# A hybrid block on one core: the order of work at the joints of its stages

## The chip, the cores and the metric

One core of one Trainium2 chip. The metric is device time in microseconds (us) of one execution. A core has five engines that run beside each other and meet through semaphores: TensorE (PE, with its weight loads PEld), VectorE (DVE), ScalarE (ACT), GpSimd (POOL) and SyncE (SP, which only issues DMAs here).

## The reference

One transformer-like block over 512 tokens of width 2048, all in fp32:

```python
h = hybrid_mixer(x, ...)            # mLSTM in chunks, and forgetting attention with 16 heads
x = layer_norm(ALPHA * x + h, ...)
h = memory_cross_attention(x, mem, w_q, w_kv, w_o)
x = layer_norm(ALPHA * x + h, ...)
h = peer_ffn(x, w_pq, sub_keys, expert_u, expert_v)
x = layer_norm(ALPHA * x + h, ...)
```

In the mixer, `merged = sigmoid(g_ml) * (h @ w_br_ml) + sigmoid(g_fx) * (y @ w_br_fx)` gates the two branches with projections of x. In `peer_ffn` each token scores two sets of 128 keys in 8 heads, picks 16 of the 16384 experts for each head (a top 16 of sums of two top 16s), softmaxes their scores to g, and computes `sum_k gelu(u_k . x) * g_k * v_k`.

## The kernel before

**Precision and the weight ring.** Every large matmul is done in three fp32r passes: hi x hi, hi x lo, lo x hi. A weight tile of 128 x 2048 floats (1 MB) is loaded by SP into a buffer `raw` (`load_raw`, L161), cast to its high part in two halves on ACT (L182), and VectorE subtracts to get the low part (L185). Both parts stand in a slot of the `ring`; later there are two slots. `shares` does this and calls the `ticks`. `group_ws` (L206) and `group_as` (L248, L249, L256) are generators that stop after every weight tile, so that another generator can be advanced in between (`mix`, `take`). A group uses three or four of five PSUM banks `mm`.

**The planner.** The instructions of an engine run in an order that a planner sets before the run: it takes those that are ready in its own reckoning of time, and among these the earlier in the program's text first. `after(i, j)` forces i behind j on their engine without a semaphore, and `ring["gate"]`, when set, puts L185 of each tile that follows behind an instruction.

**The stages.** The first 128 tokens go through the mixer, cross attention and key selection first, mixed with the products of the memory (`mem_stage`). Then 384 tokens go through the mLSTM (`second`, which starts with four groups of gates, `ml1_gates`, with raw buffers from its own pool `mlg` beside the weights' pool `wp`) and through `fx1`: four quads of four attention heads each (`fox_head`), with the q, k and v groups of the next quad after them in the program, and after the last quad four groups of gates (w_in 28 to 31). Then the ends: block 1 and blocks 2 and 3 alternate between `residual`, `norm` and `attend`. `norm` takes a function `mid` that is called right behind its last statistic (L777); `behind(g, n)` makes one that advances another generator n weight tiles, all gated behind that statistic.

**The experts, two ways.** For tokens 0 to 255 the chosen rows of `peer_u` and `peer_v` are gathered with indirect DMAs (L1026), and VectorE does the dot products (L1046) and the sums (L1062). These are the `jobs`: each tile of weights earns credit, and a job is issued on POOL and used on VectorE two or three tiles later. For tokens 256 to 511 all experts are computed densely: `next_a` takes one tile of `uT` (128 experts, a U tile), computes their activations in 48 matmuls, and after every second tile a Gelu (L1334) writes a pair of them to `ga`. 28 pairs go to DRAM (`gad`) and come back as `gb`. A matrix G of the gates per expert is built with one-hot matmuls (L1386). `stage_h` multiplies a pair with its part of G (L1427), casts it to `hph` (L150) and subtracts to `hpl` (L151). `stage_o` then runs over 16 experts at a time and two halves dh of the columns: eight V tiles of `vD` with 24 matmuls each (L1467, L1468, L1464), and adds to `acc` at the end (L1479, L1481). From expert 56 on, one U tile follows each V tile (`fill`), until all 128 are done.

Selection (`Choice.run`, `select`) of the 256 dense tokens is eight steps of small operations on VectorE; three U tiles are issued beside each of the first seven, five beside the last.

Of the kernel before, what the change touches and what calls it, by code (L numbers as in the profile page):

```python
# [10 lines left out]
F32 = mybir.dt.float32  # L11
# [4 lines left out]
AF = mybir.ActivationFunctionType  # L16
# [5 lines left out]
P = 128  # L22
# [20 lines left out]
J = 16  # L43
# [6 lines left out]
def build(tc, I, out):  # L50
    nc = tc.nc
    NC_ = PKEYS
    with ExitStack() as ctx:
# [99 lines left out]
        def load_raw(src, n=2048):  # L153
# [7 lines left out]
            nc.sync.dma_start(raw[:, :n], src)  # L161
            return raw

        ring = {"n": 0, "tiles": [wp.tile([P, 4096], F32R, tag="ring", name="ring0")]}

        def add_ring(p):
# [2 lines left out]
        def shares(raw, cost, hold=None):  # L169

            wide = len(ring["tiles"]) > 1
            for i in range(1 if wide else 2):
                ring["n"] += 1
                if wide:
                    t = ring["tiles"][ring["n"] % len(ring["tiles"])]
                    hi, lo, src = t[:, 0:2048], t[:, 2048:4096], raw
                else:
                    t, o = ring["tiles"][0], (ring["n"] % 2) * 1024
                    hi, lo = t[:, o:o + 1024], t[:, 2048 + o:3072 + o]
                    src = raw[:, i * 1024:(i + 1) * 1024]  # L180
                for c in range(0, 2048 if wide else 1024, 1024):
                    x = nc.scalar.copy(hi[:, c:c + 1024], src[:, c:c + 1024])  # L182
                    if hold is not None:
                        after(x, hold)
                s = nc.vector.tensor_sub(lo, src, hi.bitcast(F32))  # L185
                if ring.get("gate") is not None:
                    after(s, ring["gate"])
                for f in ticks:
                    f(s, cost * (2 if wide else 1))
                yield (hi, lo, 0, 2048) if wide else (hi, lo, i * 1024, 1024)  # L190
# [454 lines left out]

        def fx1(X, ypool, yT, galloc, G):
            n = 384
            with pool("fxa", side="right") as fp:
                def ft(tag, bufs, n=512):
                    return fp.tile([P, n], F32, tag=tag, bufs=bufs, name=nm(tag))  # L650
# [44 lines left out]
                for qd in range(4):  # L695
                    qs, ks, vs = {}, {}, {}

                    def ev_q(s, b, qs=qs):
                        qs[s] = ft("c", 10, n)
                        nc.scalar.activation(qs[s], b, AF.Copy, scale=FX_D ** -0.5)  # L700

                    def ev_k(s, b, ks=ks):
                        ks[s] = ft("c", 10, n)
                        nc.scalar.copy(ks[s], b)

                    def ev_v(t, b, vs=vs):
                        vs[1 + t] = ft("v", 4)
                        nc.scalar.copy(vs[1 + t], b)

                    yield from group_ws(wi[16 + 3 * qd], X, 3, ev_q)  # L710
                    yield from group_ws(wi[17 + 3 * qd], X, 3, ev_k)
                    kp, vs[0] = ft("kp", 1), ft("vp", 1)
                    nc.sync.dma_start(kp, fxk[qd])
                    nc.sync.dma_start(vs[0], fxv[qd])
                    yield from group_as(wi[18 + 3 * qd], X, 3, ev_v)
                    for s in range(4):
                        fox_head(4 * qd + s, qs[s], ks[s], kp[:, s * P:(s + 1) * P], vs, s * FX_D)
            with pool("fxg", side="right") as fp:
                sgf = []

                def ev_g(s, b):
                    t = fp.tile([P, n], F32, tag="sg", bufs=16, name=nm("sg"))
                    nc.scalar.activation(t, b, AF.Sigmoid)
                    sgf.append(t)

                for g in range(4):
                    yield from group_ws(wi[28 + g], X, 3, ev_g)

                for g in range(4):
                    def ev_b(s, b, g=g):  # L730
                        m1 = fp.tile([P, n], F32, tag="m1", bufs=3, name=nm("m1"))
                        nc.sync.dma_start(m1, mg[g * 4 + s])
                        t = sgf[g * 4 + s]
                        nc.vector.tensor_mul(t, t, b)
                        nc.vector.tensor_add(t, t, m1)
                        a, l = galloc()
                        split(a, l, t)
                        G.append((a, l))

                    yield from group_ws(I["w_br_fx"][g], yT, 3, ev_b)  # L740
# [273 lines left out]


        jobs = []
        state = {"done": 0, "credit": 0.0, "rate": 0.0, "later": [], "n": 0, "lag": 3, "mult": 1.0}
        gat = {}
        tok = {}

# [105 lines left out]
            for _ in range(n):  # L1126
                next(g, 0)

        def behind(g, n):

            def mid(last):
                ring["gate"] = last
                take(g, n)
                ring["gate"] = None

            return mid
# [66 lines left out]

        def second():
            with pool("mlg", side="right") as gp:
                raws["pools"] = [wp, gp]
                yield from ml1_gates(gp, X)
                raws["pools"] = [wp]
            yield from ml1(mls.enter_context(pool("ml1", side="right")), X, prB, hT)

# [45 lines left out]
        cs = ExitStack()  # L1256
        cpl = cs.enter_context(pool("x1c", side="right"))
        res = e1.residual(PTb, Bv, False)
        e2.norm(0, X1c, lambda: pair(cpl, "X", 16), False, behind(res, 3))
        att = e2.attend(X1c, pr1, PTc)  # L1260
        mix(res, att, 2)
        e1.norm(1, X2b, pr1, True, behind(att, 2))
# [1 line left out]
        with pool("pick1") as pp:  # L1264
# [13 lines left out]
            next(cr)  # L1278

            def mid(last):  # L1280
                c.gate = ring["gate"] = last
                take(cr, 3)
                ring["gate"] = None

            e2.norm(1, X2, lambda: pair(fpl, "X", 16), True, mid)
# [24 lines left out]
        def next_a(hold=None):  # L1310
# [19 lines left out]
                    i = nc.tensor.matmul(bank, ul[:, sl], X2[k][0], start=False, stop=k == 15)  # L1330
            abank[1:] = [i]
            if c % 2:
                ga = gap.tile([P, 512], F32, tag="ga", bufs=GA, name=nm("ga"))
                nc.scalar.activation(ga, abank[0], AF.Gelu)  # L1334
                if c // 2 in spilled:
                    nc.scalar.dma_start(gad[c // 2], ga)
                else:
                    gas[c // 2] = ga

        raws["pools"], raws["one"] = [wp, rw, wp, rw, gap], gap  # L1340
        with pool("topk", side="right") as tp:
            c = Choice(pp, tp, 2)
            steps = 0
            for w in c.run(X2, nc.sync):
                if w:
                    steps += 1
                    for i in range(5 if steps == 8 else 3):
                        next_a(w[1] if i else None)
        sel = c.sel
        rws.close()  # L1350
# [69 lines left out]
        def stage_h(c):  # L1420
# [3 lines left out]
            gt = g4[c - c % 4][:, :, c % 4:c % 4 + 2]  # L1424
            ga = gas.pop(c // 2)
            gv = ga.rearrange("p (c b t) -> p c b t", c=2, t=64)
            nc.vector.tensor_mul(gv, gv, gt.rearrange("p b c t -> p c b t"))  # L1427
            a, b = pair(mn, "hp", J + 2)
            split(a, b, ga)
            hs[c], hs[c + 1] = parts(a, b, H)  # L1430
# [3 lines left out]
        def stage_o(c0, dh, fill):  # L1434
# [3 lines left out]
            for jj in range(J // 2):  # L1438
# [5 lines left out]
                    fin_load()  # L1444
                raw = load_raw(I["vD"][c0 // 2 + jj, dh])
                for vh, vl, o, w in shares(raw, 2.0):
                    for j in range(o // 1024, (o + w) // 1024):
                        c = c0 + 2 * jj + j
                        if dh == 0 and c % 2 == 0:
                            stage_h(c)  # L1450
                        if c0 == 0 and dh == 0 and c in (10, 12):
                            late(nc.sync.dma_start(acc[c // 2 - 5], x2d[HB + c // 2 - 5].rearrange("p g c -> p (g c)")))
                    js = range(o // 1024, (o + w) // 1024)
# [45 lines left out]
        while at[0] < ahead[0]:  # L1499
# [5 lines left out]
            if at[0] == ahead[0] - 1:  # L1505
                ask_g(4)
            next_a()
        for c0 in range(0, NC_, J):
            def fill(i, c0=c0):
                if i % 2:  # L1510
# [85 lines left out]
```

## Time and profile before

| | |
|---|---|
| three runs | 4623.32, 4625.78 (median), 4626.57 us |
| the profiled execution | 4626.68 us, span 4625.0 us, granted clock 0.987 |
| TensorE busy | 4472.6 us, 97% |
| VectorE, ScalarE, GpSimd busy | 3744.9, 2228.1, 855.8 us |
| DMA | 1488.70 MB, mean 322 GB/s |

In the profile, PE slices show how much of a stretch TensorE had a matmul in flight; the granted clock is a second figure, the share of its full speed that it was given. An idle time is given with the releaser that ended it.

Where the stages lie in the span: memory products and first block to 943.9 us; mLSTM and heads of the 384 tokens to 2295 (the last heads 2227 to 2295); gates and branch of the attention, then the ends, to about 2905; selection to 3200; G to about 3440; the last U tiles to 3509; V tiles without U tiles to 3844; V and U tiles to about 4515, V tiles to 4603.

### The profile page before, as it was taken

The page shows a single profiled execution, that of the slowest core. Times are in us where ns is not written, and L with a number is a line of the kernel's source. Part 1 is how long each engine was busy: PE and PEld are TensorE (multiplying, and loading weights), DVE is VectorE, ACT ScalarE, POOL GpSimd, SP SyncE. Part 2 cuts the span into 40 slices and gives each one's busy share as a digit, 9 for nine tenths or more (in the row PEclk, how much of TensorE's full clock was granted, in tenths as well). Part 3 has the DMA queues.
Part 4 walks back from the last instruction along what each step waited for, and adds up shares of the span by engine and source line. Part 5 has one row for each costly group of instructions (what it writes and reads, how often), then busy time and mean ns, then how long its engine had stood idle before and what let it go on. Part 6 is the DMA issues. An engine that isn't in the chain of part 4 may idle for free.

```text
span 4625.0 us, 65151 instructions
## 1 busy us (share of the span) xinstructions
PE 4472.6 (97%) x25702; PEld 3991.4 (86%) x25702; DVE 3744.9 (81%) x4326; ACT 2228.1 (48%) x3029; POOL 855.8 (19%) x631
## 2 busy tenths in 40 slices
PE   8999999999999999999999999898999999999998
PEld 7888888889888899999899777898997778888886
DVE  7877677647898887888779669799988998888888
ACT  6866776645343423333323575444763433343342
POOL 1000000000122222222131000111121223334332
PEclk9999999999999999999999999999999999999999
DMA  8898889656788899888699766786989999999897
GB/s 297 322 335 327 323 318 340 253 216 214 280 335 331 329 346 344 341 332 315 248 352 355 275 236 217 272 324 250 366 353 412 399 406 379 372 369 374 357 365 298
DMA packets 244019, 1488.70 MB, mean 322 GB/s; under 512 B 26588, under 2 KB 52252, under 8 KB 75392
## 3 DMA queue, kind: packets, MB, share of 16 engines
q1 hardware_dynamic: 150384, 888.47, 51.1%
q0 software_dynamic: 81664, 561.95, 31.0%
q10 hardware_dynamic: 11664, 34.12, 1.9%
q8 instruction: 201, 3.29, 0.3%
q14 instruction: 106, 0.87, 0.1%
HBM read 1425.15 MB, written 59.29 MB: 321 GB/s over the span
## 4 chain that ended last, share of the span: by engine, by line
PE 67%; DVE 5%; DMA 3%; issue 3%; ACT 2%; POOL 0%; DVEq 0%; ACTq 0%; SPq 0%; POOLq 0%
PE mm L206 22%; PE mm L256 6%; PE mm L249 6%; PE mm L248 6%; PE pa L1330 4%; PE mm L1467 4%; PE pa L1323 4%; PE pa L1326 4%; PE mm L1468 4%; PE mm L1464 4%; DVE ring L185 2%; DVE rows L1046 1%; ACT ring L182 1%; PE sm L689 1%; PE sm L623 1%
## 5 line engine op out<-in xcount | busy, mean ns | idle before, releaser
L182 ACT CAST ring<-raw 128x1024 fp32r<-128x1024 f32 x1568 | 1598.8, 1050 | 1482.8 <-PE mm L206 464.3
L185 DVE TENSOR_TENSOR ring<-raw,ring 128x2048 fp32r<-128x2048 f32 (+1 forms) x926 | 1813.4, 1962 | 509.0 <-ACT ring L182 226.7
L206 PE MATMUL mm<-Ah,ring 128*128 128x384 f32 x2560 | 673.5, 342 | 13.9 <-ACT Ah L150 11.5
L1026 POOL DMA_INDIRECT rows<-in_peer_u,ei x256 | 330.5, 1291 | 1674.4 <-DVE rows L1046 832.1
L1026 POOL DMA_INDIRECT rows<-in_peer_v,ei x256 | 458.6, 1791 | 968.8 <-DVE x2l L1062 713.4
L1046 DVE SCALAR_TENSOR_TENSOR rows<-rows,x2l 128x2048 f32<-128x2048 f32 x256 | 584.5, 2287 | 33.2 <-DMA rows<-in_peer_u,ei 33.0
L1062 DVE SCALAR_TENSOR_TENSOR x2l<-rows,dots,x2l 128x2048 f32<-128x2048 f32 x256 | 600.9, 2347 | 10.4 <-DMA rows<-in_peer_v,ei 10.1
L1323 PE MATMUL pa<-Xh,ring 128*128 128x256 f32 x2048 | 496.9, 284 | 4.8 <-ACT ring L182 4.7
L1326 PE MATMUL pa<-Xl,ring 128*128 128x256 f32 x2048 | 493.5, 282 | 0.0
L206 PEld LDWEIGHTS mm<-Ah,ring 128*128 128x128 f32 x2560 | 464.4, 189 | 19.6 <-ACT Ah L150 12.0
L1467 PE MATMUL mm<-ring,hph 128*128 128x512 f32 x1024 | 406.4, 397 | 32.2 <-ACT ring L182 30.0
L206 PE MATMUL mm<-Al,ring 128*128 128x384 f32 x1280 | 433.3, 341 | 0.0
L1468 PE MATMUL mm<-ring,hpl 128*128 128x512 f32 x1024 | 403.1, 394 | 0.0
L1323 PEld LDWEIGHTS pa<-Xh,ring 128*128 128x128 f32 x2048 | 388.1, 189 | 9.4 <-ACT ring L182 7.1
L1326 PEld LDWEIGHTS pa<-Xl,ring 128*128 128x128 f32 x2048 | 389.4, 190 | 2.2
L249 PE MATMUL mm<-ring,Zl 128*128 128x512 f32 x832 | 328.6, 395 | 0.0
L248 PE MATMUL mm<-ring,Zh 128*128 128x512 f32 x832 | 327.7, 394 | 0.8 <-ACT ring L182 0.8
L248 PE MATMUL mm<-ring,Ah 128*128 128x512 f32 x768 | 307.2, 400 | 1.1 <-ACT ring L182 1.1
L249 PE MATMUL mm<-ring,Al 128*128 128x512 f32 x768 | 304.4, 397 | 0.0
L1330 PE MATMUL pa<-Xh,ring 128*128 128x256 f32 x2048 | 266.3, 283 | 3.0 <-DVE ring L185 3.0
L1467 PEld LDWEIGHTS mm<-ring,hph 128*128 128x128 f32 x1024 | 193.2, 189 | 83.3 <-ACT ring L182 38.2
L206 PE MATMUL mm<-Bh,ring 128*128 128x384 f32 x1024 | 261.2, 338 | 0.7 <-DVE ring L185 0.7
(393 smaller groups left out, 7153.9 us busy)
## 6 DMA issues: line engine op xcount, KB each, us to landing
raw<-in_w_in SPq DMA_DIRECT2D x256, 1024.0 KB, 6.6
raw<-in_uT SPq DMA_DIRECT2D x128, 1024.0 KB, 8.3
raw<-in_vD SPq DMA_DIRECT2D x128, 1024.0 KB, 9.5
raw<-in_w_out SPq DMA_DIRECT2D x48, 1024.0 KB, 6.3
raw<-in_peer_wq SPq DMA_DIRECT2D x48, 1024.0 KB, 4.8
raw<-in_w_xkv SPq DMA_DIRECT2D x32, 1024.0 KB, 6.5
raw<-in_w_br_ml SPq DMA_DIRECT2D x32, 1024.0 KB, 7.0
raw<-in_w_br_fx SPq DMA_DIRECT2D x32, 1024.0 KB, 7.7
```

The costliest lines, as they stand in the source:

```text
L182: x = nc.scalar.copy(hi[:, c:c + 1024], src[:, c:c + 1024])
L185: s = nc.vector.tensor_sub(lo, src, hi.bitcast(F32))
L206: i = nc.tensor.matmul(o, w, x, start=start and s % per == 0, stop=stop and s % per == per - 1)
L248: nc.tensor.matmul(banks[t], xh[:, tt], wh[:, c], start=k == 0, stop=False)
L249: nc.tensor.matmul(banks[t], xl[:, tt], wh[:, c], start=False, stop=False)
L1026: i = nc.gpsimd.indirect_dma_start(out=rows, out_offset=None, in_=I[table], in_offset=bass.IndirectOffsetOnAxis(ap=ei[t][:, k:k + 1], axis=0))
L1046: i = nc.vector.scalar_tensor_tensor(rows, rows, 1.0, tok[t]["x2l"], op0=ALU.mult, op1=ALU.mult, accum_out=d[:, k % GB:k % GB + 1])
L1062: i = nc.vector.scalar_tensor_tensor(acc, rows, d[:, GB + k % GB:GB + k % GB + 1], acc, op0=ALU.mult, op1=ALU.add)
L1323: i = nc.tensor.matmul(bank, uh[:, sl], xh, start=k == 0, stop=False)
L1326: nc.tensor.matmul(bank, uh[:, sl], xl, start=False, stop=False)
L1467: nc.tensor.matmul(banks[t][g], a[:, tt], vh[:, gs_], start=c == c0, stop=False)
L1468: nc.tensor.matmul(banks[t][g], b[:, tt], vh[:, gs_], start=False, stop=False)
```

## The change

Six edits, all to order:

1. In `fx1` the first gate group (w_in 28) becomes a generator `g0`, begun before the heads. One of its weight tiles is issued ahead of each of heads 12, 13 and 14, the fourth behind head 15. Its Sigmoids still need the pool `fxg`, which opens after the heads.
2. `behind(g, n, free=1)` advances `free` tiles before the gate is set, and only the others behind it; one norm has `free` 2. The `mid` of the last norm does the same with one of its three tiles.
3. In `second` the first weight tile of `ml1_gates` is taken before the pool's raw buffers join.
4. In the main loop the Gelu of a pair is put on a list `put`, and issued behind the casts of the next weight tile.
5. `stage_h` runs one V tile ahead: the first pair before the loop, the first pair of the next 16 experts at the seventh V tile of the second half. Its multiply is forced behind the subtraction of the present V tile.
6. Seven U tiles instead of five are issued beside the last selection, and two fewer after G.

```diff
+        put = []
...
                     x = nc.scalar.copy(hi[:, c:c + 1024], src[:, c:c + 1024])
                     if hold is not None:
                         after(x, hold)
+                while put:
+                    put.pop(0)(x)
                 s = nc.vector.tensor_sub(lo, src, hi.bitcast(F32))
...
         def fx1(X, ypool, yT, galloc, G):
             n = 384
+            sgf, gate_pool = [], []
+            def ev_g(s, b):
+                t = gate_pool[0].tile([P, n], F32, tag="sg", bufs=16, name=nm("sg"))
+                nc.scalar.activation(t, b, AF.Sigmoid)
+                sgf.append(t)
+            g0 = group_ws(wi[28], X, 3, ev_g)
...
                     for s in range(4):
+                        if qd == 3 and s < 3:
+                            yield next(g0)
                         fox_head(4 * qd + s, qs[s], ks[s], kp[:, s * P:(s + 1) * P], vs, s * FX_D)
-            with pool("fxg", side="right") as fp:
...
-                for g in range(4):
+            with pool("fxg", side="right") as gp:
+                gate_pool.append(gp)
+                yield from g0
+                for g in range(1, 4):
                     yield from group_ws(wi[28 + g], X, 3, ev_g)
...
-        def behind(g, n):
+        def behind(g, n, free=1):
             def mid(last):
+                take(g, free)
                 ring["gate"] = last
-                take(g, n)
+                take(g, n - free)
                 ring["gate"] = None
...
             with pool("mlg", side="right") as gp:
+                g = ml1_gates(gp, X)
+                yield next(g)
                 raws["pools"] = [wp, gp]
-                yield from ml1_gates(gp, X)
+                yield from g
...
-        e2.norm(0, X1c, lambda: pair(cpl, "X", 16), False, behind(res, 3))
+        e2.norm(0, X1c, lambda: pair(cpl, "X", 16), False, behind(res, 3, 2))
...
             def mid(last):
-                c.gate = ring["gate"] = last
-                take(cr, 3)
+                c.gate = last
+                take(cr, 1)
+                ring["gate"] = last
+                take(cr, 2)
                 ring["gate"] = None
...
             if c % 2:
-                ga = gap.tile([P, 512], F32, tag="ga", bufs=GA, name=nm("ga"))
-                nc.scalar.activation(ga, abank[0], AF.Gelu)
-                if c // 2 in spilled:
-                    nc.scalar.dma_start(gad[c // 2], ga)
+                def evac(x, pa=abank[0]):
+                    ga = gap.tile([P, 512], F32, tag="ga", bufs=GA, name=nm("ga"))
+                    i = nc.scalar.activation(ga, pa, AF.Gelu)
+                    if x is not None:
+                        after(i, x)
+                    if c // 2 in spilled:
+                        nc.scalar.dma_start(gad[c // 2], ga)
+                    else:
+                        gas[c // 2] = ga
+                if state["put"]:
+                    put.append(evac)
                 else:
-                    gas[c // 2] = ga
+                    evac(None)
...
-                    for i in range(5 if steps == 8 else 3):
+                    for i in range(7 if steps == 8 else 3):
                         next_a(w[1] if i else None)
...
-            nc.vector.tensor_mul(gv, gv, gt.rearrange("p b c t -> p c b t"))
+            i = nc.vector.tensor_mul(gv, gv, gt.rearrange("p b c t -> p c b t"))
+            after(i, state["s"])
...
                 for vh, vl, o, w in shares(raw, 2.0):
+                    nxt = c0 + 2 * jj + 2 if dh == 0 else c0 + J
+                    if nxt < c0 + J or (dh and jj == 6 and not last):
+                        stage_h(nxt)
                     for j in range(o // 1024, (o + w) // 1024):
                         c = c0 + 2 * jj + j
-                        if dh == 0 and c % 2 == 0:
-                            stage_h(c)
...
             next_a()
+        while put:
+            put.pop(0)(None)
+        stage_h(0)
+        state["put"] = True
         for c0 in range(0, NC_, J):
```

`state["s"]` is the subtraction (L185) of the weight tile that was issued last.

More of the change, by code (lines that the diff above doesn't have):

```diff
@@ L716, in fx1 @@
                     for s in range(4):
+                        if qd == 3 and s < 3:
+                            yield next(g0)
                         fox_head(4 * qd + s, qs[s], ks[s], kp[:, s * P:(s + 1) * P], vs, s * FX_D)
-            with pool("fxg", side="right") as fp:
[L719 to L724, printed above, removed]
-                for g in range(4):
+            with pool("fxg", side="right") as gp:
+                gate_pool.append(gp)
+                yield from g0
+                for g in range(1, 4):
                     yield from group_ws(wi[28 + g], X, 3, ev_g)
@@ L730, in ev_b @@
                     def ev_b(s, b, g=g):
-                        m1 = fp.tile([P, n], F32, tag="m1", bufs=3, name=nm("m1"))
+                        m1 = gp.tile([P, n], F32, tag="m1", bufs=3, name=nm("m1"))
                         nc.sync.dma_start(m1, mg[g * 4 + s])
@@ L1016, in build @@
         jobs = []
-        state = {"done": 0, "credit": 0.0, "rate": 0.0, "later": [], "n": 0, "lag": 3, "mult": 1.0}
+        state = {"done": 0, "credit": 0.0, "rate": 0.0, "later": [], "n": 0, "lag": 3, "mult": 1.0, "put": False}
         gat = {}
```

## The prediction

> **What bounds the kernel now.** I read the page first, then the busy time by stretches wherever TensorE's slices fell short of full, then the idle groups and the order of time around each gap.
>
> ```profile
> PE 4472.6 (97%) x25702; PEld 3991.4 (86%) x25702; DVE 3744.9 (81%) x4326; ACT 2228.1 (48%) x3029; POOL 855.8 (19%) x631
> ...
> PEclk9999999999999999999999999999999999999999
> DMA  8898889656788899888699766786989999999897
> ```
>
> TensorE is the bound almost everywhere, so an edit is worth the idle time of TensorE that it takes away, and what half clock follows a gap. The stretches in which the gaps of this change lie (columns: window, its length, then busy time of PE, PEld, DVE, ACT, POOL, then granted clock, DMA share, GB/s):
>
> ```profile
> 943.90:955.40 11.50, 0.00 (x0) 0.00 (x0) 2.29 (x1) 1.44 (x4) 1.07 (x2) 0.67 0.75 269
> 955.40:975.10 19.70, 19.66 (x97) 19.66 (x98) 8.10 (x13) 8.83 (x15) 0.00 (x0) 0.85 0.52 190
> 2227.00:2272.50 45.50, 45.50 (x266) 42.93 (x265) 37.30 (x52) 15.72 (x29) 9.57 (x8) 1.00 0.84 305
> 2272.50:2295.40 22.90, 15.77 (x67) 10.05 (x65) 10.16 (x37) 8.86 (x22) 0.94 (x1) 0.85 0.37 125
> 2698.30:2704.00 5.70, 0.01 (x1) 0.00 (x0) 5.22 (x14) 4.29 (x7) 0.00 (x0) 0.85 0.00 0
> 2704.00:2711.00 7.00, 7.00 (x20) 5.55 (x21) 6.18 (x6) 5.25 (x7) 0.00 (x0) 0.64 0.81 302
> 2882.70:2887.30 4.60, 0.00 (x1) 0.01 (x1) 4.12 (x12) 2.43 (x5) 0.00 (x0) 0.92 0.00 0
> 2887.30:2894.00 6.70, 6.70 (x16) 4.97 (x16) 3.97 (x5) 2.80 (x4) 0.00 (x0) 0.55 0.84 313
> 3181.00:3200.50 19.50, 1.43 (x3) 0.54 (x3) 19.33 (x84) 4.16 (x10) 0.00 (x0) 0.56 0.21 87
> 3440.00:3509.00 69.00, 65.71 (x552) 65.10 (x550) 50.44 (x39) 26.49 (x36) 12.32 (x11) 1.00 1.02 421
> 3509.00:3844.00 335.00, 319.79 (x1346) 251.57 (x1347) 305.51 (x263) 130.78 (x152) 74.85 (x56) 0.99 1.01 405
> 3931.00:4488.50 557.50, 539.46 (x3461) 489.99 (x3461) 469.78 (x260) 217.54 (x240) 206.54 (x92) 1.00 0.92 367
> ```
>
> The reader should see three sorts of gap: five to twenty us at stage joints, each followed by a granted clock well under 1; a stretch from 3440 to 3844 where the DMA engines are never idle; and 557 us at the end where neither DMA nor VectorE is full and TensorE still loses 18.
>
> **The change part by part.** The sum is made against the profiled execution: 4626.68 us around a span of 4625.0; the median of the three runs is 4625.78, so what comes out may be compared with it as it stands.
>
> *Gelu behind the next tile's casts.* Here is one of the waits in the last stretch: the group of idle time, then ACT, PE and the load of that tile in order of time, and the usual landing time.
>
> ```profile
> L1467 PE MATMUL mm<-ring,hph 128*128 128x512 f32 x408 | 160.4, 393 | 17.8 <-ACT ring L182 17.8
> ...
> 3911.47 0.60 ACT L1334 ACTIVATE ga<-pa 128x512 f32<-128x512 f32 x1 [11.91 <-PE pa L1330]
> 3911.96 1.98 ACT L182 CAST ring<-raw 128x1024 fp32r<-128x1024 f32 x2
> ...
> 3913.05 0.50 PE L1467 MATMUL mm<-ring,hph 128*128 128x512 f32 x1 [1.62 <-ACT ring L182]
> ...
> 3895.62 0.34 SPq L161 DMA_DIRECT2D raw<-in_vD  x1
> ...
> raw<-in_vD SPq DMA_DIRECT2D x128, 1024.0 KB, 9.5
> ```
>
> ACT stood 11.91 us before a Gelu that needed the end of the U tile, with the casts of the next V tile queued behind it, although that tile's load, issued at 3895.62, lands by the usual 9.5 us at about 3905. TensorE then waits 1.62 us for 0.5 of Gelu and one cast of 1.0. The group says 17.8 us in 11 such waits (17.8 / 1.62). The edit fixes the order: casts first. What is queued behind the Gelu then are the U tile's casts, which need the ring slot that the same U tile frees, so they lose 0.5 us of the 5.6 us of V matmuls that cover them; the Gelu's bank and its result are wanted a whole pair of tiles later. The raw buffer also comes free some 6 us earlier, so SP's next load goes out sooner. Bounds: 0, if another order of the planner puts the same wait elsewhere, to 18. I take 18, since the wait has one cause each time and the cover is seen.
>
> *The first memory gate's tile before the new pool.*
>
> ```profile
> 919.91 0.33 SPq L161 DMA_DIRECT2D raw<-in_w_in  x1
> ...
> 948.59 0.80 SPq L161 DMA_DIRECT2D raw<-in_x1T  x2
> ...
> 954.88 1.34 ACT L150 CAST Ah<-raw 128x384 fp32r<-128x384 f32 x3 [10.06 <-DMA raw<-in_x1T]
> ```
>
> TensorE does nothing from 943.9 to 955.4 because both first pieces of x1T sit in raw buffers of the pool `mlg`, which is free only at 948.6, when the last stores of the stage before have landed. After the edit the first piece takes a buffer of the weights' pool, of which the next to come free takes a load at 919.91 now; the second piece still waits. So one step, 48 matmuls, runs in the gap: 48 x 45.5/266 = 8.2 us. The gap left is 11.5 - 8.2 = 3.3 us. The slow clock behind it cost 19.7 - 97 x 0.171 = 3.1 us; what a shorter gap costs is shown elsewhere:
>
> ```profile
> 3272.28 2.07 PE L1386 MATMUL mm<-o,o 128*128 128x128 f32 x8 [2.48 <-ACT o L1385]
> ...
> 3272.30:3275.60 3.30, 3.30 (x15) 3.30 (x16) 0.00 (x0) 3.30 (x7) 0.00 (x0) 0.50 0.97 407
> ```
>
> A gap of 2.48 us was followed by 3.3 us at half clock, that is 1.7 lost, so I keep 1.7 and win 8.2 + 1.4 = 9.6. [...] Moving the first piece forward also pushes one weight load back on SP. I take 9; bounds 4 (the memory of X itself comes free late) to 14.6 (gap and clock both gone).
>
> *One or two tiles outside the norm's gate.* In front of 2704 and 2887 the stretches lose 5.7 + 7.0 x 0.36 = 8.2 and 4.6 + 6.7 x 0.45 = 7.6 us.
>
> ```profile
> 2694.25 1.05 ACT L182 CAST ring<-raw 128x1024 fp32r<-128x1024 f32 x1 [1.79 <-PE mm L249]
> ...
> 2701.66 4.49 DVE L185 TENSOR_TENSOR ring<-raw,ring 128x2048 fp32r<-128x2048 f32 x2
> ```
>
> The second of two tiles was cast by 2695.3, but both subtractions stand behind the norm's last statistic and begin at 2701.66. Freed, they fit the holes VectorE has there or push the statistics back by at most one subtraction, 2.2 us. A tile for one block of 128 rows is 12 matmuls of 512; at 319.79/1346 = 0.24 us that is 2.9 us of cover. Two freed tiles cover the 5.7; one covers 2.9 of the 4.6. Work done early is missing later, but a subtraction fewer stands between the statistic and the normalisation, so the transposes come earlier too. I take 5 and 3; bounds -4 (two statistics chains pushed back by 2.2) to 15.8. The other norms have no such gap: 0.
>
> *Gate tiles between the last heads.* While heads 12 and 13 ran, the planner had already filled TensorE with all four steps of the first gate group (45.5 of 45.5 busy); heads 14 and 15 then ran bare, 22.9 us with 15.77 busy at clock 0.85. The edit puts three of the steps ahead of heads in program order. If the planner fills greedily again, the order only decides which heads run bare, and the first step, 8.2 us, now even stands in front of head 12. Three more weight loads pass heads' loads on SP. Bounds: -8.2 (a loss of one step) to +7 (the idle part gone). I take 0, because the same cover is there in both.
>
> *Seven keys beside the last selection.* Two U tiles, 48 matmuls each, 2 x 48 x 65.71/552 = 11.4 us, move from the stretch that starts at 3440 into the 19.5 us in which TensorE waits for the selection. But VectorE has no hole there (19.33 of 19.50), and each tile brings it a subtraction and its share of jobs:
>
> ```profile
> L185 DVE TENSOR_TENSOR ring<-raw,ring 128x2048 fp32r<-128x2048 f32 x7 | 16.0, 2289 | 0.0
> L1046 DVE SCALAR_TENSOR_TENSOR rows<-rows,x2l 128x2048 f32<-128x2048 f32 x5 | 11.4, 2286 | 0.0
> ```
>
> That is 2 x (2.29 + 5/7 x 2.29) = 7.9 us by which the selection ends later. Their loads on SP and 1.4 gathers on POOL move too, into a window with DMA to spare. Net 11.4 - 7.9 = 3.5; bounds -7.9 (nothing saved later) to +11.4. I take 3.5.
>
> *Gated activations one V tile ahead.* Between 3505 and 3844 TensorE idles this much before V tiles:
>
> ```profile
> L1467 PE MATMUL mm<-ring,hph 128*128 128x512 f32 x449 | 180.6, 402 | 14.4 <-ACT ring L182 12.2 <-DVE acc L1479 1.8 <-DVE acc L1481 0.4
> ...
> L1464 PE MATMUL mm<-ring,hph 128*128 128x512 f32 x448 | 113.4, 395 | 3.4 <-DVE ring L185 3.3
> ```
>
> That is 17.8 us, most of it casts standing behind `hph`, which waits for the multiply with G. The edit puts the multiply behind the present tile's subtraction and uses it one tile later. But DMA is full here: 335 us x 405 = 135.7 MB, and the best long rate, 421 from 3440 to 3509, would need 322 us: at most 13 us to win. Between 0 and 13 I take 5, nearer the lower end, for the rate over seven stages was 405 and not 421. [...]
>
> Sum: 18 + 9 + 8 + 0 + 3.5 + 5 = 43.5; 4626.7 - 43.5 = 4583.
>
> **Rivals.**
> *The multiply becomes a chain.* Each `hph` now needs the subtraction of the tile before, a job of 2.2 us stands between, and if the planner leaves `hph` ahead of the next tile's casts on ACT, every V tile with staging takes the whole round. It exists now:
>
> ```profile
> 3527.49 1.99 ACT L182 CAST ring<-raw 128x1024 fp32r<-128x1024 f32 x2
> 3534.65 0.62 ACT L150 CAST hph<-ga 128x512 fp32r<-128x512 f32 x1 [5.17 <-DVE ga L1427]
> 3535.17 1.99 ACT L182 CAST ring<-raw 128x1024 fp32r<-128x1024 f32 x2
> ...
> 3529.51 2.29 DVE L185 TENSOR_TENSOR ring<-raw,ring 128x2048 fp32r<-128x2048 f32 x1 [1.20 <-ACT ring L182]
> 3531.72 2.28 DVE L1046 SCALAR_TENSOR_TENSOR rows<-rows,x2l 128x2048 f32<-128x2048 f32 x1
> 3533.93 1.29 DVE L1427 TENSOR_TENSOR ga<-ga,G 128x512 f32<-128x512 f32 x2
> ```
>
> From cast to cast 7.7 us, against 5.7 for the 24 matmuls of a V tile. A first half then takes 7 x 7.7 + 5.7 = 59.6 us against 335/7 = 47.9 now: +11.7 for each of the four without U tiles, and 2 us for some six tiles more: +59 in place of -5, thus 4626.7 - 38.5 + 59 = 4647. It decides when about 19 of 34 tiles fall so (38.5 / 2). For it: the planner did put `hph` first here. Against: with the product ready a tile early, the casts have a tile's time of slack.
>
> *DMA holds the stretch from 3440.* The V stages keep their 335 us, and the two U tiles less save only their bytes, 3.6 MB / 421 = 8.5 against 7.9. Then 35.6 is won: 4591. For it: share 1.01 to 1.02. Against: stalls that have nothing to do with a landing.
>
> *The Gelu edit moves casts that were not ready.* If half of the V tiles land after the U tile's last matmuls, 9 of the 18 stay: 4592. Against it stands the load above.
>
> **How the numbers follow.** Forecast 0.57, DMA 0.20, Gelu 0.08, chain 0.15. 0.2% (9.3 us) is about what a measurement of this kernel can tell from no change. The first three are all faster; from their 0.85 I take 0.04 for a shuffle by the planner that turns them into a loss, so faster is 0.81. The chain's 0.15 is split: nearly complete it is slower (0.08, with the shuffle 0.12), about half complete it is within 0.2% (0.07). The range runs from 4563, with 20 us more from the norms, the join at 955, the heads and the V stretch, to 4613, which takes in DMA, Gelu and the head's loss of 8 together and part of a chain; beyond it lies most of the chain.
>
> **What would show it.** Gelu: the idle group of L1467 in the last stretch falls from 17.8 to under 3, casts stand ahead of each Gelu. Join: x1T once at about 920, TensorE's gap before 955 near 3 us. Norms: gaps of 5.7 and 4.6 under 2. Heads: bare stretch of about 23 us still there. Selection: TensorE's wait ends 8 us later relative to its start, two U tiles fewer after 3440. V stretch: seven stages in about 330 us. I am wrong if V tiles from 3509 come 7.7 us apart, if the last 557 us do not shrink, or if stages that the diff doesn't name grow.

## The result, and the profile after

| | time | beside the kernel before | ratio, 95% interval |
|---|---|---|---|
| changed kernel, first set | 4594.6 us (median of 6, 4586.8 to 4602.5) | 4627.9 | 0.9930 [0.9917, 0.9943] |
| changed kernel, second set | 4596.3 us (median of 5, 4593.5 to 4601.0) | 4624.1 | 0.9941 [0.9927, 0.9955] |

It is 28 to 33 us faster. (Below, a gain in us that stands beside a ratio is what the ratio gives; the difference of the medians lies up to 4 us beside it.) The forecast was 4583, the range 4563 to 4613. Two executions were profiled: one of 4602.5 us (span 4600.8, the slowest of its six) and one of 4599.3 (span 4597.6). The page of the first has these lines for the three shown of before:

```profile
PE 4467.5 (97%) x25702; PEld 3993.3 (87%) x25702; DVE 3743.1 (81%) x4326; ACT 2231.7 (49%) x3029; POOL 871.0 (19%) x631
...
PEclk9999999999999999999999999899999999999998
...
DMA  8898889766798889888789766786989999999997
```

They are nearly the same: 24 us in 4600 don't show in 40 slices. The stretches show more (window, length, busy time of PE, PEld, DVE, ACT, POOL, granted clock, DMA share, GB/s), placed by the same instructions as before:

```profile
944.30:955.30 11.00, 9.19 (x52) 8.74 (x52) 4.58 (x2) 4.83 (x6) 1.08 (x2) 1.00 0.89 289
955.30:966.00 10.70, 10.70 (x51) 9.71 (x50) 4.56 (x6) 5.49 (x9) 0.00 (x0) 0.84 0.97 377
2272.50:2296.40 23.90, 16.77 (x68) 10.63 (x67) 9.93 (x35) 9.03 (x22) 0.17 (x1) 0.86 0.30 110
2701.60:2708.40 6.80, 4.73 (x19) 3.36 (x19) 6.32 (x16) 5.99 (x8) 0.00 (x0) 1.00 0.56 170
2876.00:2885.50 9.50, 4.67 (x17) 2.90 (x16) 8.83 (x17) 4.39 (x7) 0.00 (x0) 0.93 0.59 221
2911.60:2924.50 12.90, 0.01 (x1) 0.01 (x1) 2.77 (x5) 2.23 (x5) 1.25 (x1) 0.63 0.89 340
...
3496.50:3834.60 338.10, 322.77 (x1345) 258.21 (x1346) 303.32 (x262) 131.78 (x151) 86.22 (x56) 0.97 0.99 399
3921.30:4455.70 534.40, 532.54 (x3431) 485.92 (x3430) 465.43 (x257) 218.27 (x240) 185.84 (x92) 1.00 0.95 381
4574.40:4600.80 26.40, 0.49 (x3) 0.05 (x1) 22.49 (x45) 0.61 (x3) 0.00 (x0) 0.55 0.29 119
```

The gap at 944 is filled (TensorE is busy for 9.19 of 11.0). The last long stretch, which lost 18 us of 557, loses 1.9 of 534. The heads' bare stretch is as it was. Of the norms' gaps 2.1 us (6.80 - 4.73) and 4.8 (9.50 - 4.67) are left, in several pieces. New are 12.9 us at 2911 in which TensorE does nothing, a V stretch of 338 us instead of 335, and an end of 26.4 us.

The whole difference, taken between the same instructions in each profile (lengths in us; "again" is the second profile of the changed kernel, "predicted" the change that the prediction's terms give, and the last column is a better kernel, told below):

| from one event to the next | before | after | again | predicted | best1 |
|---|---|---|---|---|---|
| start to the first matmul of the memory gates | 955.4 | 944.4 | 943.8 | -9 | 943.6 |
| to the first cast of the attention's branch at 1871 | 916.3 | 926.5 | 923.6 | 0 | 920.3 |
| to the last such cast (heads) | 421.3 | 423.1 | 423.0 | 0 | 422.7 |
| to the last norm's statistics | 590.0 | 585.3 | 585.3 | -5 | 585.1 |
| to the first Gelu | 73.3 | 72.6 | 72.5 | -3 | 63.1 |
| to the end of the selection | 241.0 | 247.6 | 247.4 | +8 | 247.9 |
| to the first V tile | 311.8 | 297.0 | 297.5 | -11.4 | 298.5 |
| seven stages of V tiles | 334.7 | 338.1 | 338.3 | -5 | 335.0 |
| seven stages of V and U tiles | 645.4 | 621.7 | 621.8 | -18 | 621.7 |
| two last stages | 114.2 | 118.1 | 118.0 | 0 | 117.4 |
| last accumulation to the end | 21.6 | 26.4 | 26.4 | 0 | 19.1 |

### The profile page after: what moved, and what is told of

Same layout as the page of the kernel before. It is cut to its first block, busy times and chain, and to the rows that moved or that the text cites. A ratio compares the mean times of both kernels' runs of the same rounds, so it can differ in the third digit from the quotient of the medians.

```text
span 4600.8 us, 65219 instructions
## 1 busy us (share of the span) xinstructions
PE 4467.5 (97%) x25702; PEld 3993.3 (87%) x25702; DVE 3743.1 (81%) x4326; ACT 2231.7 (49%) x3029; POOL 871.0 (19%) x631
## 4 chain that ended last, share of the span: by engine, by line
PE 65%; DVE 6%; issue 5%; DMA 3%; POOL 1%; ACT 1%; DVEq 0%; SPq 0%; ACTq 0%; POOLq 0%
PE mm L209 22%; PE mm L259 6%; PE mm L251 6%; PE mm L252 6%; PE mm L1491 4%; PE mm L1490 4%; PE mm L1487 4%; PE pa L1343 4%; PE pa L1336 3%; PE pa L1339 3%; DVE ring L188 2%; POOL rows L1034 1%; DMA raw<-in_vD 1%; DVE rows L1054 1%; PE sm L700 1%
## 5 line engine op out<-in xcount | busy, mean ns | idle before, releaser
L1034 POOL DMA_INDIRECT rows<-in_peer_u,ei x256 | 368.6, 1440 | 1634.9 <-DVE rows L1054 791.3
L1034 POOL DMA_INDIRECT rows<-in_peer_v,ei x256 | 435.5, 1701 | 978.8 <-DVE x2l L1070 698.3
L1070 DVE SCALAR_TENSOR_TENSOR x2l<-rows,dots,x2l 128x2048 f32<-128x2048 f32 x256 | 600.7, 2347 | 11.9 <-DMA rows<-in_peer_v,ei 11.2
L1490 PE MATMUL mm<-ring,hph 128*128 128x512 f32 x1024 | 393.4, 396 | 8.3 <-ACT ring L183 5.5
L1487 PE MATMUL mm<-ring,hph 128*128 128x512 f32 x1024 | 257.6, 392 | 2.4 <-DVE ring L188 2.2
```

The source lines that it names most:

```text
L1034: i = nc.gpsimd.indirect_dma_start(out=rows, out_offset=None, in_=I[table], in_offset=bass.IndirectOffsetOnAxis(ap=ei[t][:, k:k + 1], axis=0))
L1070: i = nc.vector.scalar_tensor_tensor(acc, rows, d[:, GB + k % GB:GB + k % GB + 1], acc, op0=ALU.mult, op1=ALU.add)
L1490: nc.tensor.matmul(banks[t][g], a[:, tt], vh[:, gs_], start=c == c0, stop=False)
```

## The experiments

**The changed kernel again.** Nothing is edited.

> The changed kernel once more, with a second profile. Its first profile has two stalls that stages not named in the diff pay: TensorE waits 7.5 us at 1683.7 (a cast of a w_br_ml tile whose load took some 13 us to land) and 12.9 us at 2924.5 (a peer_wq tile). Theory 1, chance: which transfer wins a full DMA differs from execution to execution; then this profile lacks at least one of the two, or has it at another place, and the times again spread over about 15 us, the lowest near 4587. Theory 2, order: the changed issue order on SP makes both every time; then both are here again at the same place within 15 us, of the same size within 2 us.

The first stall shrank and the second stayed. TensorE's wait at 1680, in the first profile, in the second, and in two kernels whose edits lie far behind this place (edit 4 alone, edit 6 alone):

```profile
1683.68 0.69 PE L209 MATMUL mm<-Bh,ring 128*128 128x384 f32 x1 [7.47 <-ACT ring L183]
```
```profile
1680.42 0.69 PE L209 MATMUL mm<-Bh,ring 128*128 128x384 f32 x1 [3.56 <-ACT ring L183]
```
```profile
1688.76 0.69 PE L209 MATMUL mm<-Bh,ring 128*128 128x384 f32 x1 [2.73 <-ACT ring L183]
```
```profile
1687.63 0.44 PE L206 MATMUL mm<-Bh,ring 128*128 128x384 f32 x1 [3.09 <-ACT ring L182]
```

In the profiles of before, and of edits 2, 3 and 5 alone, it isn't there. So this wait doesn't need the edits, and it comes and goes from one execution to the next; the stretch that holds it is up to 10 us longer. Whether edit 3 makes it more frequent isn't settled: of the nine profiles with edit 3 five show it (2.37 to 7.47 us), of the five without it two. The wait at 2921 is 12.82 and 12.90 us: that one is made. The kernels without edit 5 (12.94) and without edit 1 (12.84) have it too.

**Edit 4 alone in the kernel before.**

```diff
+                while put:
+                    put.pop(0)(x)
                 s = nc.vector.tensor_sub(lo, src, hi.bitcast(F32))
...
-                nc.scalar.activation(ga, abank[0], AF.Gelu)
+                put.append(evac)
```

> The kernel before with edit 4 alone (Gelu behind the next tile's casts). Theory 1, the prediction: the 17.8 us of idle time before V tiles in the last stretch go, nothing else moves: 18 to 24 us faster, 4604 to 4610 beside 4628. Rival, the gain of 24 us that the changed kernel shows between 3844 and 4489 needs the staging one tile ahead as well: then 9 us or less here, and V tiles still wait for casts.

4605.0 us beside 4624.1, ratio 0.9961 [0.9947, 0.9974], 18 us. The groups of TensorE's idle time in the last long stretch, of this kernel and of the changed one:

```profile
L1478 PE MATMUL mm<-ring,hph 128*128 128x512 f32 x376 | 146.9, 391 | 0.0
```
```profile
L1490 PE MATMUL mm<-ring,hph 128*128 128x512 f32 x392 | 152.9, 390 | 0.0
```

The 17.8 us are gone with this edit alone, and the stretch from 3844 is 20.9 us shorter; the rival falls. In order of time in the changed kernel, the V tile's casts now end before TensorE wants them, and the Gelu waits where nobody waits for it:

```profile
3894.51 1.05 ACT L183 CAST ring<-raw 128x1024 fp32r<-128x1024 f32 x1 [0.81 <-PE mm L1491]
3901.95 0.60 ACT L1348 ACTIVATE ga<-pa 128x512 f32<-128x512 f32 x1 [6.39 <-PE pa L1343]
```

**Edit 3 alone.**

```diff
+                g = ml1_gates(gp, X)
+                yield next(g)
                 raws["pools"] = [wp, gp]
-                yield from ml1_gates(gp, X)
+                yield from g
```

> The kernel before with edit 3 alone (first tile of the memory gates ahead of the pool's raw buffers). Theory 1: 9 to 11 us faster, 4617 to 4619 beside 4628, first matmul of the gates near 944 instead of 955. Rival: the 11 us are given back at 1683 because transfers now meet there; then TensorE stands 7 to 8 us there in this profile as well, and the time is 0 to 2 us faster.

4617.4 beside 4624.1, ratio 0.9985 [0.9976, 0.9994]: 7 us, under the 9 to 11 of theory 1. Its profile, of the fastest of its eleven executions, has the first gate matmul at 942.4, 13 us early, and no wait at 1683. Since that wait comes and goes, this alone would not refute the rival; but the interval of the ratio, 3 to 11 us, lies above the rival's 0 to 2. The gap is filled, and behind what is left of it the clock does not fall:

```profile
942.40:953.50 11.10, 8.54 (x49) 8.18 (x47) 4.58 (x2) 4.11 (x6) 1.07 (x2) 1.00 0.91 303
953.50:962.00 8.50, 7.98 (x40) 7.05 (x41) 4.17 (x5) 4.56 (x8) 0.00 (x0) 1.00 0.97 368
```

**Edit 2 alone, and the order on SP.**

```diff
-                ring["gate"] = last
-                take(g, n)
+                take(g, free)
+                ring["gate"] = last
+                take(g, n - free)
```

> The kernel before with edit 2 alone (one or two tiles outside the norm's gate). Theory 1, the prediction: 8 us faster, both gaps (5.7 and 4.6 us) under 2. What the changed kernel's two profiles show instead is 9 us won between the third and the sixth statistics and about 5 of it left at the first Gelu, because the last load of peer_wq goes out at the same time as before (its buffer is memory that the selection of block 1 frees) and TensorE then waits 12.8 us for it. Theory 2: the same here, 4 to 6 us faster. In this kernel that load keeps its place ahead of the third load of uT on SP; if the 12.8 us come from the place on SP alone, no such wait is here and all of 8 to 9 us stays.

4610.0 beside 4623.9, ratio 0.9973 [0.9963, 0.9984]: 12.5 us, more than predicted. In its profile 6.4 us are won up to the last norm's statistics (583.6 instead of 590.0) and 8.7 from there to the first Gelu (64.6 instead of 73.3); 6.3 are lost again before the first V tile, which was not traced. Only a part of this is what the prediction counted. Of the first gap, 5.69 us, 2.06 are left in two pieces (0.76 and 1.30). Of the second, 4.63, there are still 2.86 (2.13 and 0.73). The greater part of the 8.7 comes from a wait that the prediction does not list: in the kernel before, TensorE waits 4.17 us for the load `keysT`. SP issues this load 49.5 us behind the last norm's statistics; with edit 2 alone it is 39.0 us, with one load of uT fewer ahead of it. Here are the wait and the issue before, then the issue with edit 2 alone:

```profile
2944.79 2.05 PE L1002 MATMUL sm<-keysT,qT 128*128 128x128 f32 x8 [4.17 <-DMA keysT<-in_keysT]
...
2932.51 0.88 SPq L979 DMA_DIRECT2D keysT<-in_keysT  x2
```
```profile
2910.99 0.87 SPq L979 DMA_DIRECT2D keysT<-in_keysT  x2
```

All five profiles without edit 2 have this wait (3.00 to 4.17 us), none of the nine with it. Before, the clock behind it was 0.50 over 6.6 us, so that wait and clock together cost an estimated 4.17 + 6.6 / 2 = 7.5 us.

The wait of 12.9 us is 3.4 here. What differs, in order of time, first the changed kernel (TensorE, ACT and SP), and what SP waited for there (total, times, longest):

```profile
2924.49 0.58 PE L209 MATMUL mm<-Xh,ring 128*128 128x256 f32 x1 [12.90 <-ACT ring L183]
...
2923.40 1.99 ACT L183 CAST ring<-raw 128x1024 fp32r<-128x1024 f32 x2 [10.67 <-DMA raw<-in_peer_wq]
...
2888.48 24.42 SPq L161 DMA_DIRECT2D raw<-in_uT  x3
2913.00 0.41 SPq L161 DMA_DIRECT2D raw<-in_peer_wq  x1
```
```profile
SPq L161 <- DVE ei L1020: 14.8, 1, 14.8
```

The same of edit 2 alone:

```profile
2907.32 0.38 PE L206 MATMUL mm<-Xh,ring 128*128 128x256 f32 x1 [3.38 <-ACT ring L182]
...
2881.21 4.03 SPq L161 DMA_DIRECT2D raw<-in_uT  x2
2901.22 0.33 SPq L161 DMA_DIRECT2D raw<-in_peer_wq  x1
```
```profile
SPq L161 <- DVE eq L957: 15.9, 1, 15.9
```

Both loads wait for memory that the first selection still holds. Alone, peer_wq stands third in the queue and leaves when `eq` is done; in the changed kernel a third uT load stands ahead of it, waits 14.8 us for `ei`, which comes later, and holds it up. Edit 2 alone does not make this order; nor are edits 1 and 5 needed for it (without them SP waits 14.2 and 14.0 us for `ei`); which of 3, 4 and 6 is needed was not run.

The order forced back in the changed kernel:

```diff
+            if raws.get("lead") is not None:
+                after(i, raws["lead"])
...
+                    if steps == 1:
+                        first = raws["last"][0]
+                    raws["lead"] = first if steps == 2 else None
```

> The changed kernel with one order forced on SP: the three loads of uT for the second step of the selection stand behind the third load of peer_wq in the queue, so that none of them holds it up. Theory 1, place in the queue: the wait of 12.8 us before the gates' last peer_wq tile falls to some 3 us, as in the run with edit 2 alone, and the kernel is 7 to 9 us faster than the changed kernel. Rival, the buffer of peer_wq itself is late: the wait keeps at least 9 us, and the time is within 3 us of the changed kernel's.

```profile
2908.49 0.58 PE L212 MATMUL mm<-Xh,ring 128*128 128x256 f32 x1 [3.88 <-ACT ring L186]
```

The wait is 3.88 us and the stretch to the first Gelu 64.7 instead of 72.5, as theory 1 has it. The time is not: 4593.7, ratio 0.9932 [0.9919, 0.9946], which can't be told from the changed kernel's. Of the 7.8 us won in its profile, 2.0 are lost again by the first V tile, and then comes

```profile
3483.90:3826.00 342.10, 322.42 (x1350) 256.01 (x1350) 307.67 (x265) 133.97 (x153) 86.01 (x57) 0.98 0.99 399
```

that is 342.1 us in the V stretch instead of 338.3, the stretch in which edit 5 works.

**Edit 5 alone, and the changed kernel without it.**

```diff
-                        if dh == 0 and c % 2 == 0:
-                            stage_h(c)
+                    nxt = c0 + 2 * jj + 2 if dh == 0 else c0 + J
+                    if nxt < c0 + J or (dh and jj == 6 and not last):
+                        stage_h(nxt)
```

> The kernel before with edit 5 alone (gated activations one V tile ahead). Theory 1, the prediction's term: 5 us faster, seven stages from 3509 in about 330 us instead of 335. Rival, DMA holds the stretch: 0, the seven stages keep 335 us. Second rival: the first tile of each 16 experts waits for its hpl 3.2 us in three of the stages, as in the changed kernel, on top of a stretch that DMA holds: 3 to 10 us slower.

4627.9 beside 4624.1, ratio 1.0005 [0.9996, 1.0014]: no gain, and by the bound of the prediction no change. In its profile the seven stages of V tiles take 343.9 us, 9.2 more than before; the seven stages with U tiles give 7.7 back, and the two last lose 5.2.

> The changed kernel without edit 5 (gated activations again beside their own V tile). Theory 1, the prediction: 5 us slower than the changed kernel. Theory 2, from the run with edit 5 alone (9.2 us lost in the seven stages from 3509, 7.7 won with the U tiles, 6.3 lost in the stage at 4490): with the Gelu edit in place there is nothing left for it to win with the U tiles, so the changed kernel is 2 to 6 us faster without it; no stage then has the wait of 3.2 us for hpl.

4590.4, ratio 0.9929 [0.9916, 0.9942]. The times don't tell it from the changed kernel; the stretches do. TensorE's groups from the first V tile on, with edit 5 alone, and in the changed kernel without it:

```profile
L1470 PE MATMUL mm<-ring,hpl 128*128 128x512 f32 x450 | 171.4, 404 | 9.5 <-DVE hpl L151 9.5
L1469 PE MATMUL mm<-ring,hph 128*128 128x512 f32 x450 | 170.6, 402 | 11.3 <-ACT ring L182 5.1 <-ACT hph L150 3.7 <-DVE acc L1483 1.2
```
```profile
L1488 PE MATMUL mm<-ring,hph 128*128 128x512 f32 x449 | 180.6, 402 | 14.4 <-ACT ring L183 11.9 <-DVE acc L1500 2.1 <-DVE acc L1502 0.5
L1489 PE MATMUL mm<-ring,hpl 128*128 128x512 f32 x448 | 177.9, 397 | 0.0
```

The waits for casts fall from 11.9 to 5.1, and 9.5 us of waits for `hpl` and 3.7 for `hph` take their place. The stretches, of the same two:

```profile
3505.80:3849.70 343.90, 322.75 (x1350) 256.07 (x1350) 308.03 (x264) 134.14 (x153) 87.69 (x57) 0.98 0.98 395
```
```profile
3481.30:3816.00 334.70, 320.26 (x1345) 251.59 (x1346) 304.83 (x264) 130.09 (x151) 71.30 (x56) 0.99 1.01 405
```

344 us with, 335 without (334.7 before), and the DMA share is 0.98 with it, 1.01 without. One of the three waits for `hpl`, VectorE and TensorE in the changed kernel:

```profile
3595.68 0.69 DVE L1448 TENSOR_TENSOR gb<-gb,G 128x512 f32<-128x512 f32 x1
3596.29 2.29 DVE L1054 SCALAR_TENSOR_TENSOR rows<-rows,x2l 128x2048 f32<-128x2048 f32 x1
...
3598.50 2.29 DVE L188 TENSOR_TENSOR ring<-raw,ring 128x2048 fp32r<-128x2048 f32 x1
3600.70 0.68 DVE L1448 TENSOR_TENSOR gb<-gb,G 128x512 f32<-128x512 f32 x1
3601.30 0.69 DVE L151 TENSOR_TENSOR hpl<-gb,hph 128x512 fp32r<-128x512 f32 x1
...
3602.04 1.22 PE L1491 MATMUL mm<-ring,hpl 128*128 128x512 f32 x2 [3.17 <-DVE hpl L151]
```

The multiply of the first pair comes only behind the last stage's accumulation, and its `hpl` behind a job, a subtraction and the next multiply.

**Edit 6 alone.**

```diff
-                    for i in range(5 if steps == 8 else 3):
+                    for i in range(7 if steps == 8 else 3):
```

> The kernel before with edit 6 alone (seven keys beside the last selection). Theory 1, the prediction: the selection's wait ends 8 us later, the first V tile comes 3.5 us earlier, 3.5 us faster. Theory 2: the first V tile comes 7 to 9 us earlier, as in the changed kernel (6.5 lost before the selection's transposes, 14.5 won behind), and 4.8 us are given back at the end, where the statistics of the gathered rows now stand behind the last accumulation on VectorE: 2 to 4 us faster, with the time from the last accumulation to the end 26.4 us instead of 21.6.

4622.2 beside 4623.9, ratio 0.9997 [0.9989, 1.0006]. The selection takes 6.6 us longer and the way from there to the first V tile 16.2 less, so 9.6 are won by then; the two last stages give back 3.8 and the end 4.9. TensorE waits for only 1.3 us in the two last stages; the rest is work, for 16 matmuls of U tiles have moved into them from the stretch ahead (240 of them instead of 224; TensorE is busy for 116.7 us instead of 114.2). Before, the U tiles run until 4537, not until about 4515. The end on VectorE, this kernel and then before:

```profile
4593.43 2.48 DVE L1481 TENSOR_TENSOR acc<-acc,mm 128x512 f32<-128x512 f32 x4 [4.41 <-PE mm L1464]
4595.83 2.46 DVE L1091 BATCH_NORM_STATS2 fst<-x2l 128x6 f32<-128x512 f32 x4
```
```profile
4593.08 2.47 DVE L1091 BATCH_NORM_STATS2 fst<-x2l 128x6 f32<-128x512 f32 x4
...
4602.79 2.48 DVE L1481 TENSOR_TENSOR acc<-acc,mm 128x512 f32<-128x512 f32 x4 [2.22 <-PE mm L1464]
```

The gathered rows' statistics have moved from ahead of the last accumulation to behind it, and with them their normalisation: two U tiles moved to where a tile earns less credit, so the last job comes one tile later (the kernel's factor for the credit is 0.65 beside the selection and 1.5 behind it).

**The end mended in the changed kernel.**

```diff
-        state["mult"] = 0.86
+        state["mult"] = 0.87
```

> The changed kernel with one number changed: the main loop's credit for a tile is 0.87 instead of 0.86, so that the jobs that edit 6 left over are issued earlier. Theory 2 of the run with edit 6 alone: the statistics of the gathered rows stand ahead of the last accumulation again, the end comes 21.6 us behind it instead of 26.4, 4.8 us faster than the changed kernel. Rival: more jobs in the main loop's tiles cost VectorE what the end wins: no difference.

4588.0, ratio 0.9928 [0.9916, 0.9941]. In its profile the end is 19.1 us, 7.3 less than in the changed kernel, since the gathered rows are now done before the last accumulation:

```profile
4559.01 2.48 DVE L1084 SCALAR_TENSOR_TENSOR x2l<-x2l,fst,lw 128x1024 f32<-128x1024 f32 x2
4563.14 2.48 DVE L1504 TENSOR_TENSOR acc<-acc,mm 128x512 f32<-128x512 f32 x4 [1.65 <-PE mm L1487]
```

No stretch ahead of it grew, so the rival falls by the profile; the intervals of the times still overlap those of the changed kernel.

**The changed kernel without edit 1.**

```diff
-                        if qd == 3 and s < 3:
-                            yield next(g0)
```

> The changed kernel without edit 1 (all gate steps again behind the last heads in program order). Theory 1, the prediction: no difference (0, bounds -8.2 to +7). Rival, from the profiles so far, in which the stretch from the first heads to the last branch cast takes 421.5 to 423.0 us with edit 1 and 419.5 to 421.3 without: 2 to 3 us faster without edit 1. The bare stretch beside the last two heads stands in both.

4595.2, ratio 0.9937 [0.9923, 0.9950], the changed kernel's own. The heads take 421.6 us instead of 423.0, and 2.1 are lost behind them. Edit 1 is worth nothing that these runs can tell.

**All mends together.** Edit 5 taken out, the order on SP and the credit as above; and then without edit 1 too.

> The changed kernel without edit 5, with the loads of uT for the second step of the selection behind the third load of peer_wq, and with the main loop's credit at 0.87. If the three add up: 4 us (edit 5) and 8 (order on SP) and 5 to 7 (end), some 18 us faster than the changed kernel, 4575 to 4580. Rival: what is won at the selection is lost again where DMA is full, from 3500 on, since the V tiles there come at the rate of the transfers: some 10 us only, 4585.

> The same as best1, without edit 1 too. If edit 1 costs 2 to 3 us, this is 2 to 3 us faster than best1; if it costs nothing, the same within 3 us.

4573.4 us, ratio 0.9886 [0.9871, 0.9902], and 4572.7, ratio 0.9889 [0.9874, 0.9905], beside 4622.5: 49 to 53 us faster than before, and 22 faster than the changed kernel without edit 1 in the same set (4595.2). By the ledger's last column the three add up: 9.4 (72.5 to 63.1) + 3.3 (338.3 to 335.0) + 7.3 (26.4 to 19.1) = 20. The V stretch is 335.0 us although it begins 12 us sooner than in the changed kernel, so what the order on SP wins is not lost at DMA when edit 5 is out. Why the stretch grew to 342 with it was not traced further.

## Why the prediction came out as it did

The forecast was 11.6 us below the measured time. The direction and the range held, and so did the mechanisms of three terms (Gelu, join, heads); those of the norms, the seven keys and the gated activations were incomplete or wrong. That the total came out so near is in part luck: against the predicted column, the second profile wins 12.7 us more in four stretches and 28.7 less in seven. One of the signs by which the prediction said it would be wrong did come: stages that the diff does not name grew, the way to 1871 by 7 to 10 us and the end by 4.8. Step by step:

- **Gelu, 18.** Right in mechanism and size: 18 alone, 20.9 in that profile's stretch, waits 17.8 to 0.0. Of the 23.6 in the changed kernel, about 2 are the 16 matmuls that edit 6 moved out of the stretch. The load landed early enough, as argued; the rival that half of the casts were not ready is refuted.
- **Join, 9.** Right: 7 by the times, 11 to 13 by the profiles. Its clock term was one value where there are several (below).
- **Norms, 8.** For the first gap the mechanism was right (6.4 won alone, 5 forecast). For the second it was not shown: where a gap under 2 us was forecast, 2.86 are left with edit 2 alone and 4.40 in the changed kernel (2.13 and 2.27), and the 8.7 us won behind the statistics are for the greater part the wait for `keysT`, which the prediction did not have. So the 12.5 alone are partly luck. In the changed kernel only 5.4 are left (4.7 to the statistics, 0.7 to the first Gelu). The step that failed is the one not taken: the gates' tiles were followed on ACT and VectorE, and not on SP, where the same edit, together with the others, let a load that must wait pass a load that is needed. That costs 8 to 9 us, and the same step missed the gain at `keysT`.
- **Heads, 0.** Right, for the reason given: the same bare stretch, 16.77 busy of 23.9.
- **Seven keys, 3.5.** The 7.9 lost were 6.4 to 6.6; the 11.4 won were 14.3 to 16.2. With edit 6 alone TensorE's busy time on that way falls from 296.6 to 282.6 us, for 96 matmuls fewer, and its idle time from 15.2 to 13.1. The 2.6 of busy time beyond the 11.4 fit the clock: before, it was 0.50 for 3.4 us at 3272 and 0.51 for 3.4 us at 3347, an estimated 3.4 us lost; in the first profile of the changed kernel, where the busy time on that way is 282.8 us, it was 1.00 from 3212 to 3495. Wrong was to end the account at the first V tile: the jobs that the two tiles carry are due in the last stage, and their being late costs 4.9 us at the end; another 3.8 come in the two last stages, most of them matmuls moved there from the stretch ahead. Alone, edit 6 can't be told from nothing (1.4 us by the ratio).
- **Gated activations, 5.** Wrong in sign: 3.5 us lost in the changed kernel's stretch, 9.2 alone. The rival of full DMA came nearer: the stretch takes 332 to 335 us in every kernel without edit 5, and its 4591 is nearer to the result than the forecast; that DMA and nothing else holds these 335 us is argued, not shown. That the edit brings waits of its own, 3.17 us three times, because a pair staged across the border of 16 experts meets the accumulation on VectorE, neither had. The rate of 421 GB/s from which the bound of 13 us was worked out didn't come either: over the V stretches shown it was 395 to 405 GB/s. The rival of the multiply chain is refuted: first halves took at most 53.7 us in the changed kernel's profile, not 59.6.
- **Not in the sum:** 7 to 10 us on the way to 1871, with the wait at 1683, which the two profiled executions had and the one of before had not.

With the terms as they stood in the second profile: 11.6 - 7.3 - 1.7 + 4.7 + 0.8 - 6.4 + 14.3 - 3.6 + 23.6 - 3.8 - 4.8 = 27.4, which is 4625.0 - 4597.6.

## What to carry to other kernels

An edit that moves weight tiles moves their loads and their side jobs too: follow each of them to the end of the kernel, on every queue, and look for a load that waits for memory standing ahead of one that doesn't. Before a change of the engines' order, look whether the transfers already fill the stretch: in the V stretch, where the DMA share was 1.01 before, edit 5 alone won nothing (343.9 us, 334.7 before) and added waits. A wait of the profile that a second execution doesn't have is no term of a sum, so a second profile of the same kernel is worth a run.

## What the runs showed of the hardware

A gap of the same length can cost differently within one execution and from one to the next. The three waits for `hpl` are 3.17 to 3.18 us each; behind them, in the second profile of the changed kernel, 5.79 us of TensorE look like this:

```profile
3598.81:3604.60 5.79, 5.79 (x25) 4.72 (x26) 5.79 (x6) 2.09 (x3) 1.15 (x1) 1.00 0.94 377
3693.98:3699.77 5.79, 5.79 (x14) 4.54 (x15) 5.79 (x6) 2.08 (x3) 1.15 (x1) 0.50 0.93 371
3791.10:3796.89 5.79, 5.79 (x18) 4.62 (x19) 5.79 (x6) 2.08 (x3) 1.14 (x1) 0.71 0.94 380
```

25, 14 and 18 matmuls in the same time, at clocks 1.00, 0.50 and 0.71; behind the first of these in the other profile of the same kernel the clock was 0.50:

```profile
3602.04:3607.83 5.79, 5.79 (x14) 4.58 (x15) 5.79 (x6) 2.08 (x3) 1.15 (x1) 0.50 0.95 378
```

So in these 5.79 us the same gap was followed by no half clock (1.00), by an estimated 3.4 us of it (0.71: 5.79 x 2 x (1 - 0.71)), and by half clock all through (0.50). What decides between the three these rows don't show.

The prediction priced the gap of 3.3 us that it left at the join at the 1.7 us of clock that one gap of 2.48 us had cost. That price is one draw of several: in the second profile three gaps of 3.18 us cost an estimated 0, 2.9 and 1.7 us of clock in the 5.79 us behind them (half of 5.79 and of 3.4).
